# A hybrid decoder layer: output norm by pairs of heads, last residual rows on TensorE, an earlier SiLU of z, transposes copied by VectorE

## The chip, the cores and the metric

The kernel runs on one core of one Trainium2 chip. The metric is the device time of one execution in microseconds (us); lower is better. Before the change three runs gave 1408.13, 1408.22 and 1409.44 us, median 1408.22.

A core has five engines, each with its own instruction stream executed in order: TensorE (PE in the profile, with PEld for its weight loads), VectorE (DVE), ScalarE (ACT), GpSimd (POOL) and SyncE (SP, which here only starts transfers). They meet through semaphores. Matmul results land in the accumulator memory (PSUM, tiles named ps_...), all else lives in on-chip SBUF tiles.

## The reference, cut to what matters

One layer of a decoder for 256 prompt tokens and 8 samples of 4 tokens, 288 tokens together, width 2048:

```python
mix = concat[A(z_A), B(z_B), C(z_C)]          # z = rms_norm(x) @ w_in
x   = x + rms_norm(mix @ w_out, g_post_mix)
x   = x + rms_norm(relu(rms_norm(x) @ w_up) ** 2 @ w_down, g_post_mlp)
```

A is dilated attention, C sliding-window attention, B a gated delta rule with 4 heads of 128. The change touches three pieces of B and the last line:

```python
o = rms_norm(o, dn_g) * silu(b_z)             # B's output norm, per head, and its gate z
S = S * gl + kd^T @ v_new                     # state; for the samples written to state_delta_s
y = x + rms_norm(u @ w_down, g_post_mlp)      # the last residual, 16 rows of 128 x 288
```

## The kernel before, in words

All tensors are held transposed: 128 features on the partitions, 288 tokens along the free dimension, so a "row" of the residual is a tile of 128 x 288 and the layer has 16 of them. Every weight matmul is done in three passes: the weights come by DMA in pieces (`base_wr`), ACT casts a piece to a rounded high part (`base_wh`, line 384), DVE subtracts to get the low part (`base_wl`, line 326), and PE adds high x high, high x low and low x high into one accumulator (line 316). The pieces run one after the other: `w_in` (88 pieces), `w_o1` (32, over the first 12 of the 16 mixed rows, those of A and C and of nothing that B makes), `w_o2` (8, over B's 4 rows), then `w_up` and `w_dn`. At piece i the program casts piece i+3 and makes the low part of piece i+2.

B's own work is written as generators (`g_group`, `g_chunk`, `g_bdec`, `g_bfin` ...). A generator does a step and yields an estimated latency; between pairs of matmuls `advance` takes each generator that is due and emits its next step. So the order on each engine is fixed when the program is built, by those latencies, and the hardware keeps it.

The places that the change touches:

- `g_group(kind)`: convolved queries (kind 0), keys (1) and values (2) get their SiLU on ACT, between two loads of ACT's function table. In kind 2 the same function also takes the SiLU of the gate z (`zs`, 128 x 1152) and, after the second table load, multiplies it by the norm's gain `dng`.
- `inverse4`: the triangular inverse of a chunk. PE transposes `U` into a PSUM tile (`ps_mx`), ACT copies it to `A` (`b_cAA`), DVE makes the masked start matrices `b_cM` from it.
- `g_bdec`: the samples' chunk. At its end it multiplies the 8 tiles of old state `s0` (`st_s`, 128 x 512) by their decay on POOL; much later, during the `w_up` pieces, `fill_out` adds PE's update on DVE and stores the tile.
- `g_bfin`: B's output norm. It must be done before the last piece of `w_o1`, since `split_mix` turns its result (`base_mix` rows 6 to 9) into the high and low parts that `w_o2` reads.
- The tail after the last matmul: a sum of squares by two matmuls with a matrix of ones, ACT's Ln and Exp, three DVE instructions (`newton`) that refine 1/sqrt into `ml_m_r`, and then for each row of y a multiplication by `ml_m_r` and an addition of the residual row, DVE on rows 0 to 10 in groups, POOL on rows 15 down to 11 one at a time, and the stores from SP and ACT.

PSUM has 8 buffers: 2 `ps_acc`, 2 `ps_lx`, 4 `ps_mx`. A buffer is reused when its last reader is done.

## Time and profile before

| | |
|---|---|
| median of 3 runs | 1408.22 us |
| the profiled execution's own time | 1408.04 us |
| its span, first to last instruction | 1406.3 us |
| busy: PE / DVE / ACT / POOL | 1365.2 / 789.7 / 589.7 / 137.7 us |
| mean granted TensorE clock | 0.992 |

The profile shows one execution. Busy time is time in which an engine executes. Timeline rows read: start, duration, engine, source line, operation, out<-in, shape, how many merged, and in brackets the idle time just before with the instruction that ended it. Rows of the windows view give, for a stretch A:B, its length and each engine's busy time with the number of instructions, then the granted TensorE clock (1.00 is full speed) and the use of the DMA engines. Group rows end with busy us, mean ns of one | idle before.

### The profile page before, as it was taken

Reading aid. Unit: us, or ns where it says so; the run is one execution under the profiler, and the core shown is the slowest. Engines: PE = TensorE matmul, PEld = TensorE weight load, DVE = VectorE, ACT = ScalarE, POOL = GpSimd, SP = SyncE. Lnnn points to the kernel's source line nnn. Section 1 sums busy time; section 2 is a strip of 40 time slices with the busy share of each in tenths; the row PEclk is TensorE's granted clock in tenths of the full one; section 3 lists DMA queues with packets and bytes.
Section 4 is the critical chain, followed back from the end, with each engine's and each line's share of the span. In section 5 each row is a group of like instructions: output and inputs, shape, how many; then the busy total and the mean of one; then the engine's idle time right before and its main releaser. Section 6 shows DMA issues by size and latency. Waiting matters only on the chain.

```text
span 1406.3 us, 26913 instructions
## 1 busy us (share of the span) xinstructions
PE 1365.2 (97%) x11293; PEld 1301.2 (93%) x11293; DVE 789.7 (56%) x1302; ACT 589.7 (42%) x901; POOL 137.7 (10%) x203
## 2 busy tenths in 40 slices
PE   8999999999989999999999999999999999999994
PEld 7888887789978989899999999999999999999994
DVE  7543455546876667976433555443555444555555
ACT  7443434434772346633333334333433333434441
POOL 1111110102440050000000000000000000000114
PEclk9999999999999999999999999999999999999997
DMA  7779888744423536555555454545454545455541
GB/s 273 286 289 355 315 315 320 278 155 155 143 84 93 157 98 234 171 180 186 180 166 165 150 172 158 180 154 177 153 176 157 174 161 169 157 173 164 167 151 67
DMA packets 71065, 262.12 MB, mean 186 GB/s; under 512 B 8128, under 2 KB 10560, under 8 KB 70944
## 3 DMA queue, kind: packets, MB, share of 16 engines
q1 hardware_dynamic: 68544, 254.72, 53.8%
q0 software_dynamic: 1536, 4.89, 0.9%
q8 instruction: 88, 1.44, 0.4%
q10 hardware_dynamic: 864, 0.80, 0.2%
q14 instruction: 33, 0.27, 0.1%
HBM read 253.14 MB, written 7.24 MB: 185 GB/s over the span
## 4 chain that ended last, share of the span: by engine, by line
PE 91%; DVE 5%; ACT 2%; issue 1%; POOL 1%; DMA 0%; SPq 0%; POOLq 0%; DVEq 0%; ACTq 0%
PE ps_acc L316 35%; PE ps_mx L316 33%; PE ps_lx L316 21%; DVE base_wl L326 1%; PE ps_mx L320 1%; POOL ml_y L326 1%; DVE base_mix L326 1%; DMA base_wr<-w_in 0%; DVE b_cM L326 0%; DVE base_xl L335 0%; DVE cv_sq L335 0%; ACT base_xh L1534 0%; DVE base_xl L326 0%; DVE x_sa L326 0%; ACT base_mix L323 0%
## 5 line engine op out<-in xcount | busy, mean ns | idle before, releaser
L384 ACT CAST base_wh<-base_wr 128x1024 fp32r<-128x1024 f32 (+1 forms) x374 | 385.2, 1032 | 551.7 <-PE ps_mx L316 207.2
L326 DVE TENSOR_TENSOR base_wl<-base_wr,base_wh 128x1024 fp32r<-128x1024 f32 (+1 forms) x376 | 458.4, 1233 | 75.6 <-ACT base_wh L384 74.3
L316 PE MATMUL ps_acc<-base_xh,base_wh 128*128 128x288 f32 (+1 forms) x1056 | 322.1, 306 | 1.0 <-DVE at_z L335 0.8
L316 PE MATMUL ps_acc<-base_xl,base_wh 128*128 128x288 f32 (+1 forms) x1056 | 310.8, 296 | 0.7 <-DVE base_xl L326 0.7
L316 PE MATMUL ps_acc<-base_xh,base_wl 128*128 128x288 f32 x1040 | 303.9, 295 | 2.8 <-DVE base_wl L326 2.8
L316 PEld LDWEIGHTS ps_acc<-base_xh,base_wh 128*128 128x128 f32 (+1 forms) x1056 | 197.5, 187 | 19.0 <-issue 15.9
L316 PE MATMUL ps_mx<-ml_big,base_wh 128*128 128x288 f32 x1024 | 203.3, 294 | 0.0
L316 PEld LDWEIGHTS ps_acc<-base_xl,base_wh 128*128 128x128 f32 (+1 forms) x1056 | 197.5, 187 | 2.0 <-DVE base_xl L326 1.0
L316 PEld LDWEIGHTS ps_acc<-base_xh,base_wl 128*128 128x128 f32 x1040 | 194.9, 188 | 3.7 <-DVE base_wl L326 3.7
L316 PEld LDWEIGHTS ps_mx<-ml_big,base_wh 128*128 128x128 f32 x1024 | 164.1, 188 | 0.0
L316 PE MATMUL ps_mx<-ml_big,base_wl 128*128 128x288 f32 x512 | 150.9, 295 | 0.0
L316 PE MATMUL ps_mx<-base_xh,base_wh 128*128 128x288 f32 x480 | 142.3, 296 | 0.0
L316 PE MATMUL ps_mx<-base_xl,base_wh 128*128 128x288 f32 x480 | 141.6, 295 | 0.0
L316 PE MATMUL ps_mx<-base_xh,base_wl 128*128 128x288 f32 x480 | 141.1, 294 | 0.0
L316 PE MATMUL ps_lx<-base_xh,base_wh 128*128 128x288 f32 x400 | 122.7, 307 | 5.9 <-ACT base_xh L323 5.9
L316 PE MATMUL ps_lx<-base_xh,base_wl 128*128 128x288 f32 x400 | 116.1, 296 | 3.4 <-DVE base_wl L326 3.4
L316 PE MATMUL ps_lx<-base_xl,base_wh 128*128 128x288 f32 x400 | 118.9, 300 | 0.0
L316 PE MATMUL ps_acc<-ml_big,base_wh 128*128 128x288 f32 x512 | 101.8, 294 | 0.0
L316 PE MATMUL ps_lx<-ml_big,base_wh 128*128 128x288 f32 x512 | 101.8, 294 | 0.0
L316 PEld LDWEIGHTS ps_mx<-ml_big,base_wl 128*128 128x128 f32 x512 | 96.2, 188 | 0.0
L316 PEld LDWEIGHTS ps_mx<-base_xh,base_wl 128*128 128x128 f32 x480 | 90.4, 188 | 0.0
L316 PEld LDWEIGHTS ps_mx<-base_xl,base_wh 128*128 128x128 f32 x480 | 90.1, 188 | 0.1
(413 smaller groups left out, 1815.8 us busy)
## 6 DMA issues: line engine op xcount, KB each, us to landing
base_wr<-w_up SPq DMA_DIRECT2D x128, 512.0 KB, 3.7
base_wr<-w_dn SPq DMA_DIRECT2D x128, 512.0 KB, 3.8
base_wr<-w_in SPq DMA_DIRECT2D x86, 512.0 KB, 4.3
kv_kv<-kv_k SPq DMA_DIRECT2D x24, 896.0 KB, 7.8
kv_kv<-kv_v SPq DMA_DIRECT2D x28, 768.0 KB, 7.0
base_wr<-w_o SPq DMA_DIRECT2D x32, 384.0 KB, 3.1
base_wr<-w_o SPq DMA_DIRECT2D x8, 512.0 KB, 4.5
ml_big<-xT SPq DMA_DIRECT2D x4, 576.0 KB, 4.9
```

The source lines that it names most:

```text
L316: PE.matmul(out, lhsT=lhsT, rhs=rhs, start=start, stop=stop, **kw)
L320: PE.transpose(out, in_, idn)
L326: eng.tensor_tensor(out=out, in0=a, in1=b, op=op)
L384: S.copy(out=p["wh"], in_=p["wr"])
```

## The change

It has five parts.

1. The SiLU of z moves from the values' group to the keys' group, between that group's own table loads, and the multiplication by `dng` leaves ACT (it is folded into the norm's last instruction).
2. `inverse4` copies the transposed `U` on DVE instead of ACT (one copy of 128 x 512 for each of the two chunks).
3. The decay of the sample states leaves POOL: instead of 8 multiplications there and 8 additions on DVE, DVE does 4 fused multiply-adds of 128 x 128 per tile in `fill_out`.
4. `g_bfin` works by pairs of heads. POOL no longer takes part; DVE multiplies z by o, reads the sums of squares straight from PSUM, and does three fused instructions of 128 x 576 per pair. ACT's four PSUM copies and its second Square are gone, Exp is done per pair. `split_mix` of B's rows is issued in two halves.
5. The tail: PE adds the residual for rows 9 to 15. Seven PSUM buffers are first filled with identity x residual row, then identity x scaled row is added, ACT copies the sum back and stores it (3, 2 and 2 rows per store). DVE scales rows 9 to 15, then scales and adds rows 0 to 8 itself, stored by SP in groups of 4, 2, 2 and 1. POOL has no part in it.

The diff, without the constant `BY_PE = (9, 10, 11, 12, 13, 14, 15)`:

```diff
@@ g_group
-        if kind == 2:
+        if kind == 1:
             zs = mixp[:, 6:10, :]
             act(zs, zs, AF.Silu)
+            done.add("siluz")
         ...
         S.preload_act_table_set("natural_log_exp_and_others")
-        if kind == 2:
-            act(zs, zs, AF.Identity, scale=dng)
-            done.add("siluz")
@@ inverse4
-        S.copy(out=A, in_=p)
+        V.tensor_copy(out=A, in_=p)
@@ g_bdec
-        fill.update(vn=vn, kd=kds, s0=s0)
-        for i in range(8):
-            ...
-            tt(G, t, t, bc(sc, [P, 4, P]), ALU.mult)
-            yield FP
+        fill.update(vn=vn, kd=kds, s0=s0, eg=eg3)
@@ fill_out
-        tt(V, t, t, p.rearrange("p (n x) -> p n x", n=4), ALU.add)
+        for n in range(4):
+            k = 8 * h + 4 * q + n
+            stt(V, t[:, n, :], t[:, n, :], fill["eg"][:, k:k + 1], p[:, n * P:(n + 1) * P], ALU.mult, ALU.add)
@@ g_bfin
-        act(sq, B["o"], AF.Square)
-        tt(G, zs, zs, B["o"], ALU.mult)
-        ...
-            act(r[:, h, :], p, AF.Ln, bias=epsc[:, 0:1], scale=1.0 / P)
-            S.copy(out=t[:, h, :], in_=p)
-        ...
-        act(r, r, AF.Exp, scale=-0.5)
-        act(sq, r, AF.Square)
-        tt(G, zs, zs, r, ALU.mult)
-        stt(V, t, t, EPS * P, sq, ALU.add, ALU.mult)
-        ts(V, t, t, -0.5 / P, ALU.mult, 1.5, ALU.add)
-        tt(V, zs, zs, t, ALU.mult)
+        pairs = (slice(0, 2), slice(2, 4))
+        for a in pairs:
+            act(sq[:, a, :], B["o"][:, a, :], AF.Square)
+        tt(V, zs, zs, B["o"], ALU.mult)
+        yield 1.5
+        for a in pairs:
+            for h in range(a.start, a.stop):
+                p = mx(T)
+                mm(p, ones, sq[:, h, :])
+                act(r[:, h, :], p, AF.Ln, bias=epsc[:, 0:1], scale=1.0 / P)
+                cur["bf", h] = p
+            act(r[:, a, :], r[:, a, :], AF.Exp, scale=-0.5)
+            if a.start == 0:
+                yield 0.4
+        for a in pairs:
+            for h in range(a.start, a.stop):
+                stt(V, t[:, h, :], cur.pop(("bf", h)), EPS * P, r[:, h, :], ALU.add, ALU.mult)
+            ta, ra, za = t[:, a, :], r[:, a, :], zs[:, a, :]
+            stt(V, ta, ta, -0.5 / P, ra, ALU.mult, ALU.mult)
+            stt(V, ta, ta, 1.5, ra, ALU.add, ALU.mult)
+            stt(V, za, za, dng, ta, ALU.mult, ALU.mult)
+            yield 2.5
         while "o1" not in done:
             yield 1.0
-        split_mix(range(N_P1, KT))
+        split_mix(range(N_P1, N_P1 + 2))
+        yield 0.8
+        split_mix(range(N_P1 + 2, KT))
@@ the tail
-        p = mx(T)
+        p = new_acc()[:, 0:T]
         ...
+        banks = {m: new_acc()[:, 0:T] for m in BY_PE}
+        for m in BY_PE:
+            mm(banks[m], ident, orow(m), stop=False)
         newton(V, r, t, p, r, 1.0 / D, EPS)
-        for steps in (((V, 0, 4, SP), (G, 15, 1, S)), ((V, 4, 2, SP), (G, 14, 1, S)), ((V, 6, 3, SP), (G, 13, 1, S)),
-                      ((V, 9, 1, SP), (G, 12, 1, S)), ((V, 10, 1, SP), (G, 11, 1, S))):
-            ...
+        def by_pe(lo, n):
+            for m in range(lo, lo + n):
+                mm(banks[m], ident, y[:, m, :], start=False)
+                S.copy(out=y[:, m, :], in_=banks[m])
+            out(S, lo, n)
+        scale(9, 2)
+        scale(11, 1)
+        by_pe(9, 3)
+        scale(12, 4)
+        by_pe(12, 2)
+        by_pe(14, 2)
+        for lo, n in ((0, 4), (4, 2), (6, 2), (8, 1)):
+            scale(lo, n)
+            add(lo, n)
+            out(SP, lo, n)
```

Three places where the instructions of an engine stand in another order. The names carry buffer numbers, which differ by one or two between the programs; so do source lines.

ACT at the values' group, before the change (`base_mix` is z here, `cv_ca` a convolved value, `base_pm` holds `dng`):

```order
L648 ACT_TABLE_LOAD
L323 ACTIVATE base_mix_65<-base_mix_65 128x1152
L323 ACTIVATE cv_ca_4442<-cv_ca_4442 128x312
L323 ACTIVATE cv_ca_4517<-cv_ca_4517 128x312
L323 ACTIVATE cv_ca_4610<-cv_ca_4610 128x312
L323 ACTIVATE cv_ca_4753<-cv_ca_4753 128x312
L655 ACT_TABLE_LOAD
L323 ACTIVATE base_mix_65<-base_mix_65,base_pm_62 128x1152
L384 CAST base_wh_4816<-base_wr_4665 128x768
L384 CAST base_wh_4858<-base_wr_4744 128x768
L812 COPY b_cAA_32_4899<-ps_mx_4903 128x512
L812 COPY b_cAA_35_4930<-ps_mx_4934 128x512
```

and after it:

```order
L649 ACT_TABLE_LOAD
L324 ACTIVATE cv_ca_4443<-cv_ca_4443 128x312
L324 ACTIVATE cv_ca_4518<-cv_ca_4518 128x312
L324 ACTIVATE cv_ca_4611<-cv_ca_4611 128x312
L324 ACTIVATE cv_ca_4754<-cv_ca_4754 128x312
L657 ACT_TABLE_LOAD
L385 CAST base_wh_4815<-base_wr_4666 128x768
L385 CAST base_wh_4857<-base_wr_4745 128x768
L385 CAST base_wh_4948<-base_wr_4781 128x768
```

Both instructions on z are gone from between the table load and the cast of the next weight piece, and both copies are gone from behind it.

DVE in the output norm, before the change (`sp_ft`, `sp_fa`, `sp_fb` are the norm's temporaries, `base_oext` takes a finished row of `w_o1`):

```order
L326 TENSOR_TENSOR base_wl_6120<-base_wr_5962,base_wh_6119 128x768
L326 TENSOR_TENSOR base_wl_6155<-base_wr_6006,base_wh_6154 128x768
L1538 COPY base_mix_65<-ps_lx_6160 128x288
L326 TENSOR_TENSOR base_wl_6189<-base_wr_6082,base_wh_6188 128x768
L335 SCALAR_TENSOR_TENSOR sp_ft_6137<-sp_ft_6137,sp_fa_6109 128x1152
L332 TENSOR_SCALAR sp_ft_6137<-sp_ft_6137 128x1152
L326 TENSOR_TENSOR base_wl_6216<-base_wr_6123,base_wh_6215 128x768
L1538 COPY base_oext_66<-ps_acc_6221 128x288
L326 TENSOR_TENSOR base_mix_65<-base_mix_65,sp_ft_6137 128x1152
L326 TENSOR_TENSOR base_wl_6245<-base_wr_6158,base_wh_6244 128x768
```

and after it:

```order
L336 SCALAR_TENSOR_TENSOR sp_ft_6109<-ps_mx_6137,sp_fb_6108 128x288
L336 SCALAR_TENSOR_TENSOR sp_ft_6109<-ps_mx_6140,sp_fb_6108 128x288
L336 SCALAR_TENSOR_TENSOR sp_ft_6109<-sp_ft_6109,sp_fb_6108 128x576 x2
L336 SCALAR_TENSOR_TENSOR base_mix_65<-base_mix_65,base_pm_62,sp_ft_6109 128x576
L327 TENSOR_TENSOR base_wl_6120<-base_wr_5961,base_wh_6119 128x768
L327 TENSOR_TENSOR base_wl_6164<-base_wr_6005,base_wh_6163 128x768
L336 SCALAR_TENSOR_TENSOR sp_ft_6109<-ps_mx_6151,sp_fb_6108 128x288
L336 SCALAR_TENSOR_TENSOR sp_ft_6109<-ps_mx_6154,sp_fb_6108 128x288
L336 SCALAR_TENSOR_TENSOR sp_ft_6109<-sp_ft_6109,sp_fb_6108 128x576 x2
L336 SCALAR_TENSOR_TENSOR base_mix_65<-base_mix_65,base_pm_62,sp_ft_6109 128x576
L1537 COPY base_mix_65<-ps_lx_6169 128x288
L327 TENSOR_TENSOR base_wl_6189<-base_wr_6081,base_wh_6188 128x768
```

The norm's DVE work now stands two to three weight pieces earlier, around the low parts `wl_6120` and `wl_6164` and ahead of `wl_6189`, in ten instructions where there were three.

DVE in the tail, before the change:

```order
L326 TENSOR_TENSOR ml_y_8004<-ml_y_8004,ml_m_r_15129 128x1152
L326 TENSOR_TENSOR ml_y_8004<-ml_y_8004,base_mix_65 128x1152
L326 TENSOR_TENSOR ml_y_8004<-ml_y_8004,ml_m_r_15129 128x576
L326 TENSOR_TENSOR ml_y_8004<-ml_y_8004,base_mix_65 128x576
L326 TENSOR_TENSOR ml_y_8004<-ml_y_8004,ml_m_r_15129 128x864
```

and after it:

```order
L327 TENSOR_TENSOR ml_y_8022<-ml_y_8022,ml_m_r_15147 128x576
L327 TENSOR_TENSOR ml_y_8022<-ml_y_8022,ml_m_r_15147 128x288
L327 TENSOR_TENSOR ml_y_8022<-ml_y_8022,ml_m_r_15147 128x1152 x2
L327 TENSOR_TENSOR ml_y_8022<-ml_y_8022,base_mix_65 128x1152
L327 TENSOR_TENSOR ml_y_8022<-ml_y_8022,ml_m_r_15147 128x576
L327 TENSOR_TENSOR ml_y_8022<-ml_y_8022,base_mix_65 128x576
L327 TENSOR_TENSOR ml_y_8022<-ml_y_8022,ml_m_r_15147 128x576
L327 TENSOR_TENSOR ml_y_8022<-ml_y_8022,base_mix_65 128x576
```

Seven rows are scaled first (576, 288 and the first 1152), for PE; then come rows 0 to 8, scaled and added.

## The prediction

> **What bounds the kernel now.** I read the chain of waits first, then PE's rows that stood idle, then the windows around them, then the rows of the engines that PE waited for.

> ```profile
> PE 91%; DVE 5%; ACT 2%; issue 1%; POOL 1%; DMA 0%; SPq 0%; POOLq 0%; DVEq 0%; ACTq 0%
> ```

> PE carries 91% of the chain that ended last. An edit on another engine is worth only the time that PE stands idle for it, or what stands behind the last matmul. The change touches three such places, and all else that it moves lies beside PE.

> ```profile
> 421.85 0.66 PE L320 MATMUL ps_mx<-base_cst,cv_ca 128*128 128x128 f32 x2 [4.18 <-DVE b_cB L326]
> 518.89 0.40 PE L316 MATMUL ps_acc<-base_xh,base_wl 128*128 128x288 f32 x1 [1.24 <-DVE base_wl L326]
> 522.72 0.40 PE L316 MATMUL ps_lx<-base_xh,base_wl 128*128 128x288 f32 x1 [1.18 <-DVE base_wl L326]
> 525.92 0.40 PE L316 MATMUL ps_lx<-base_xh,base_wl 128*128 128x288 f32 x1 [0.54 <-DVE base_wl L326]
> 1386.61 0.75 PE L316 MATMUL ps_mx<-ml_sq,base_cst 128*128 128x288 f32 x2 [0.59 <-ACT ml_sq L323]
> ```

> PE waits 4.18 us for DVE at the values' group (place A), 1.24 + 1.18 + 0.54 = 2.96 us for low parts at the output norm (place B), and after 1387.36 it has nothing more to do while the residual is added (place C). The profiled execution took 1408.04 us, 1.74 more than its span of 1406.3 and 0.18 less than the median.

> **Place A: the SiLU of z and the two copies.**

> ```profile
> 414.24 1.17 ACT L323 ACTIVATE base_mix<-base_mix 128x1152 f32<-128x1152 f32 x1
> 415.31 1.51 ACT L323 ACTIVATE cv_ca<-cv_ca 128x312 f32<-128x312 f32 x4
> 418.13 1.25 ACT L323 ACTIVATE base_mix<-base_mix,base_pm 128x1152 f32<-128x1152 f32 x1
> 419.30 1.55 ACT L384 CAST base_wh<-base_wr 128x768 fp32r<-128x768 f32 x2
> ...
> 420.14 0.96 DVE L326 TENSOR_TENSOR base_wl<-base_wr,base_wh 128x768 fp32r<-128x768 f32 x1 [4.48 <-ACT base_wh L384]
> 421.62 1.12 DVE L335 SCALAR_TENSOR_TENSOR b_cU<-ps_mx,b_bP,b_cA 128x128 f32<-128x128 f32 x4
> 431.81 0.28 DVE L326 TENSOR_TENSOR b_cM<-ps_mx,base_cst 128x128 f32<-128x128 f32 x1
> ```

> Start to start, z's SiLU holds ACT for 415.31 − 414.24 = 1.07 us and its product with `dng` for 419.30 − 418.13 = 1.17. Without both, the cast starts at 417.06 instead of 419.30, and DVE's low part, which stands in order ahead of `b_cB`, 2.24 us earlier. So PE's stall falls from 4.18 to about 1.95 us. Whether that reaches the end depends on who is the bound next.

> ```profile
> 417.66:421.85 4.19, 0.01 (x2) 0.03 (x1) 1.71 (x3) 3.65 (x5) 2.52 (x7) 0.90 0.11 40
> 421.85:427.20 5.35, 5.07 (x21) 4.64 (x22) 5.16 (x19) 1.32 (x2) 0.00 (x0) 0.50 0.23 74
> 427.20:434.40 7.20, 7.04 (x168) 6.55 (x167) 7.04 (x18) 1.67 (x2) 0.00 (x0) 0.96 0.35 101
> ...
> 432.15 0.72 PE L316 MATMUL ps_mx<-b_cM 32*32 32x32 f32 x62 [0.16 <-DVE b_cM L326]
> ```

> Behind the stall PE runs 5.35 us at a granted clock of 0.50, with few long matmuls (21). DVE is busy for 5.16 of those 5.35 us and 7.04 of the next 7.20, and at 432.15 PE waits for DVE again. So DVE, not the slow clock, sets the pace from 420.14 to 432: it starts 2.24 us earlier, but it now also makes the two copies of 128 x 512 out of PSUM, each 0.68 us alone and about 0.60 from start to start (the `st_s` row under place B; `b_cB` to `b_cU`: 421.02 to 421.62). Gain at A: 2.24 − 1.2 = 1.0; I take **0.9**, since POOL is busy for 2.52 us in the first window and may hold DVE a little. Bounds: 0 if DVE's extra work comes in front of something that PE needs at once; above, the case in which PE is the bound there (a rival, below).

> The moved SiLU adds its 1.07 us to ACT in the keys' group. The next low part there comes later by as much:

> ```profile
> 382.54 1.23 DVE L326 TENSOR_TENSOR base_wl<-base_wr,base_wh 128x1024 fp32r<-128x1024 f32 x1 [1.10 <-ACT base_wh L384]
> 380.00:400.00 20.00, 19.91 (x143) 19.09 (x142) 16.31 (x29) 13.37 (x25) 9.86 (x21) 1.00 0.40 125
> ```

> It would be done at 383.77 + 1.07 = 384.8. Low parts are made two pieces ahead, and PE was idle for only 0.09 of these 20 us, so I cost this at nothing; with the cover gone, at most 1.1.

> **Place B: the output norm.**

> ```profile
> 498.09 0.96 DVE L326 TENSOR_TENSOR base_wl<-base_wr,base_wh 128x768 fp32r<-128x768 f32 x1 [1.14 <-ACT base_wh L384]
> ...
> 510.60 2.89 DVE L326 TENSOR_TENSOR base_wl<-base_wr,base_wh 128x768 fp32r<-128x768 f32 x1
> 513.42 2.19 DVE L335 SCALAR_TENSOR_TENSOR sp_ft<-sp_ft,sp_fa 128x1152 f32<-128x1152 f32 x1
> 515.64 1.48 DVE L332 TENSOR_SCALAR sp_ft<-sp_ft 128x1152 f32<-128x1152 f32 x1
> 517.04 1.79 DVE L326 TENSOR_TENSOR base_wl<-base_wr,base_wh 128x768 fp32r<-128x768 f32 x1
> 519.13 1.83 DVE L326 TENSOR_TENSOR base_mix<-base_mix,sp_ft 128x1152 f32<-128x1152 f32 x1
> ...
> 509.99 2.68 POOL L326 TENSOR_TENSOR base_mix<-base_mix,sp_fb 128x1152 f32<-128x1152 f32 x1 [4.42 <-ACT sp_fb L323]
> 512.63 7.11 POOL L326 TENSOR_TENSOR st_s<-st_s,st_eg 128x512 f32<-128x512 f32 x4
> ```

> One low part of 128 x 768 takes 0.96 us alone (498.09) and 2.89 and 1.79 while POOL computes (from 509.99 on). That, with the norm's three instructions (2.19 + 1.48 + 1.83 = 5.5 us) in front, is why PE waits. After the change POOL has no norm product and no decay, only two masks that the order puts ahead, so DVE runs at its own speed. What it gets:

> ```profile
> L326 DVE TENSOR_TENSOR base_mix<-base_mix,ml_big 128x576 f32<-128x576 f32 x5 | 3.8, 758 | 0.2
> L335 DVE SCALAR_TENSOR_TENSOR ml_r<-ps_lx,ml_m_r 128x288 f32<-128x288 f32 x1 | 0.5, 458 | 0.2 <-ACT ml_m_r L323 0.2
> L326 DVE TENSOR_TENSOR st_s<-st_s,ps_mx 128x512 f32<-128x512 f32 x4 | 2.6, 681 | 0.0
> ...
> 515.10 0.29 PE L316 MATMUL ps_acc<-base_xh,base_wl 128*128 128x288 f32 x1
> ```

> Four instructions of 128 x 288 from PSUM (0.46), six of 128 x 576 (0.76) and one of 128 x 1152 (1.36, the row 1389.89 under C): 1.8 + 4.6 + 1.4 = 7.8 us, 2.3 more than before, but on a free DVE. By the new order the product goes ahead at about 499.9, when POOL made it before; the first pair follows near 505 to 508, the low parts 6120 by 508.9 and 6164 by 509.8, the second pair to 512.9, low part 6189 by 514.1. In the old trace PE begins six matmuls on each of these parts, at 0.40 us each, the third at 515.10 (the first two at 510.3 and 512.7). So the tightest (6120 and 6189) have 1.4 and 1.0 us left, and from 514.1 DVE runs ahead of PE. The sums of squares now stay in PSUM until DVE has read them, in `ps_mx` buffers that `w_o1` (`ps_acc`, `ps_lx`) does not use. All three stalls go: **2.9**, with 3.0 as the most. Downward, with that slack gone, each us that DVE is later costs PE a us; if all 7.8 us came in front of the low parts, the place would lose 7.8 − 3.0 = 4.8 and its clock with it.

> [...]

> **The additions of the sample states** become four instructions per tile: 1.12 us (421.62) in place of 0.68, 0.44 x 8 = 3.5 us on DVE. Cover:

> ```profile
> 607.95 0.46 DVE L335 SCALAR_TENSOR_TENSOR ml_m_t<-ps_mx,ml_m_r 128x288 f32<-128x288 f32 x1 [6.07 <-ACT ml_m_r L323]
> ```

> The additions are spread over the first `w_up` pieces, where DVE stands idle for 6.07 us in front of this row alone. Nothing; with no cover, one tile in front of a waited-for part costs 0.44.

> **Place C: the tail.**

> ```profile
> 1389.89 1.36 DVE L326 TENSOR_TENSOR ml_y<-ml_y,ml_m_r 128x1152 f32<-128x1152 f32 x1
> 1391.28 1.83 DVE L326 TENSOR_TENSOR ml_y<-ml_y,base_mix 128x1152 f32<-128x1152 f32 x1
> ...
> 1390.02 1.88 POOL L326 TENSOR_TENSOR ml_y<-ml_y,ml_m_r 128x288 f32<-128x288 f32 x1 [8.86 <-DVE ml_m_r L335]
> 1402.38 0.88 POOL L326 TENSOR_TENSOR ml_y<-ml_y,base_mix 128x288 f32<-128x288 f32 x1
> ...
> 559.52 1.13 PE L316 MATMUL ps_lx<-ml_sq,base_cst 128*128 128x288 f32 x4
> ```

> Both engines work from 1389.89 to 1403.26, and the last store lands 3.04 us later, at the span's end. They slow each other: DVE's 1152 row takes 1.83 in place of 1.36 once POOL has begun. After the change DVE has, at their own lengths, 0.76 (rows 9, 10), 0.46 (11), 1.36 (12 to 15), 2 x 1.36 (0 to 3), 4 x 0.76 (4 to 7) and 2 x 0.46 (8): 9.3 us. Independent neighbours overlap by some 0.1 us (the seven here about 0.6), dependent ones stand 0.03 apart, so the last addition ends near 1389.89 + 9.3 − 0.5 = 1398.7 instead of 1403.26: 4.56 us. PE's part must end before that. One fp32 matmul of 128 x 288 is two instructions, so the row 559.52 holds two of them: 0.57 us each. The seven fills, 4.0 us, stand from 1387.4 beside Ln, Exp and the refinement; the seven additions follow the scaled rows, which are there from 1391 and complete near 1392.3, and end near 1395.3, ACT's last copy (some 0.4) at 1396. At half clock they would end near 1399.5 and take 0.8 of the gain, but between fills and additions PE hardly stands idle. The stores (three from ACT behind its copies, four from SP, for five each) have nothing queued behind them. The store of row 8 is as small as the last one before, but 2.36 MB now leave in a shorter time: 0 to 1 us more for the landing, I take 0.15. **4.4**, bounds 2 and 4.6.

> **Sum.** 0.9 + 2.9 + 4.4 = 8.2; 1408.04 − 8.2 = 1399.8, plus 0.18 to the median: **1400.0 us**.

> **Rivals.**

> *All of A comes through (1396).* If PE and its clock, not DVE, bound 421.85 to 432, the whole 2.24 counts, and a stall of 1.95 us may leave the clock up, as stalls of 1.24 did elsewhere:

> ```profile
> 500.00:520.00 20.00, 18.76 (x135) 18.11 (x134) 12.50 (x10) 10.90 (x17) 15.57 (x10) 1.00 0.27 81
> ```

> The 5.35 us at 0.50 would then give 2.7 back: 4.9 in place of 0.9. For it speaks the 0.50; against it DVE's 5.16 of 5.35 us. [...]

> *The stores bound the tail (1402).* If the last store waits for those ahead of it, C gives half, 2.2. For it: 16 rows end within 5 us; against it: in the old tail the DMA engines were used to 0.41.

> *The norm's stalls only move (1403 to 1406).* DVE's ten instructions delay low parts 6120 to 6189 past their slack, and new stalls eat the 2.9 or a little more: 1408.2 − 0.9 − 4.4 = 1402.9, and up to 3 us above that. For it: 7.8 us of DVE work between 505 and 513; against it: DVE idled for 5.44 us before 504.49 and 2.98 before 510.23 there.

> ```profile
> 504.49 0.46 DVE L1538 COPY base_mix<-ps_lx 128x288 f32<-128x288 f32 x1 [5.44 <-PE ps_lx L316]
> 510.23 0.46 DVE L1538 COPY base_mix<-ps_lx 128x288 f32<-128x288 f32 x1 [2.98 <-PE ps_lx L316]
> ```

> *Slower (1411).* The same mechanism whole: the first pair starts late, all 7.8 us stand in front of a low part, PE idles over 4 us, and the clock falls as behind 417.66: 5.35 us at 0.50 and 0.58 more in the next window (0.04 x 7.20 / 0.5) cost 3.0. If PE at place A waits for DVE's copies too, 0.4 is left there. 4.8 + 3.0 − 0.4 − 4.4 = +3.0. It decides once B loses more than the 5.3 us of A and C. For it speaks that DVE already has 5.5 us of norm work where PE now waits; against it, DVE's gaps above.

> **Chances.** Forecast 0.62, all of A 0.12, stores 0.14, moved stalls 0.08, slower 0.04. The forecast's own range is 1398 to 1402; to hold 8 in 10 it must reach into the first and third rival: **1396.5 to 1403.5**. A measurement here tells about 0.2% (2.8 us, so 1405.4 and 1411.0) from no change. Half of the moved stalls and a little of the slower case lie within it: faster 0.91, same 0.05, slower 0.04.

> **What would show it.** A: PE's stall before the values' transposes about 2 us instead of 4.2, clock not at 0.50, DVE without idle up to the masked start matrices. B: no PE row from 510 to 530 that waits for `base_wl`, low parts at 0.96 instead of 2.89, POOL without 128 x 1152. C: the last DVE addition 8.8 us after the refinement, the span's end 3 us behind it, no POOL row. Wrong: a PE stall on a low part near 512 to 516; low parts still near 2 us; a DVE gap in the tail; a last store that lands over 4 us after the last addition.

## The result and the profile after

The changed kernel takes **1398.99 us** (median of 4 runs, 1398.06 to 1400.43) against 1408.33 us before (4 runs beside it, 1408.13 to 1409.44): a ratio of 0.9935, 95% interval 0.9923 to 0.9946. Two later measurements gave 1400.21 (0.9945, 0.9932 to 0.9957) and 1399.81 us (0.9944, 0.9931 to 0.9956). So it is 8 to 9 us faster. The first trace of it has a span of 1397.8 us, 8.5 less than the trace before the change.

To see where that went, both programs need the same landmarks. VectorE copies each finished mixed row out of PSUM (line 1538 before, 1537 after). The first, fourth, sixth, eleventh and fifteenth of these copies in the stretch serve here. VectorE's timeline before and, behind the dots, after (start, duration, instruction):

```profile
412.71 0.45 DVE L1538 COPY base_mix<-ps_acc 128x288 f32<-128x288 f32 x1
440.57 0.46 DVE L1538 COPY base_mix<-ps_lx 128x288 f32<-128x288 f32 x1 [0.63 <-PE ps_lx L316]
459.26 0.45 DVE L1538 COPY base_mix<-ps_acc 128x288 f32<-128x288 f32 x1
528.35 0.46 DVE L1538 COPY base_oext<-ps_lx 128x288 f32<-128x288 f32 x1 [0.38 <-PE ps_lx L316]
```

```profile
412.17 0.45 DVE L1537 COPY base_mix<-ps_acc 128x288 f32<-128x288 f32 x1
439.02 0.46 DVE L1537 COPY base_mix<-ps_lx 128x288 f32<-128x288 f32 x1 [0.63 <-PE ps_lx L317]
458.99 0.45 DVE L1537 COPY base_mix<-ps_acc 128x288 f32<-128x288 f32 x1
504.21 0.46 DVE L1537 COPY base_mix<-ps_lx 128x288 f32<-128x288 f32 x1 [2.29 <-PE ps_lx L317]
524.37 0.46 DVE L1537 COPY base_oext<-ps_lx 128x288 f32<-128x288 f32 x1 [2.61 <-PE ps_lx L317]
```

| stage, by landmarks of before | before | after | gain |
|---|---|---|---|
| 0 to 412.71 (nothing changed but the moved SiLU) | 412.71 | 412.17 | 0.54 |
| 412.71 to 440.57, values' group and start of the inverse (A) | 27.86 | 26.85 | 1.01 |
| 440.57 to 459.26, rest of the inverse | 18.69 | 19.97 | -1.28 |
| 459.26 to 504.49 | 45.23 | 45.22 | 0.01 |
| 504.49 to 528.35, output norm (B) | 23.86 | 20.16 | 3.70 |
| 528.35 to the span's end, with the tail (C) | 877.95 | 873.43 | 4.52 |

The first line is no gain: the twelve later traces, of kernels with and without the moved SiLU, have 412.10 to 413.48 there. B and C delivered a little more than forecast. A delivered its 1.0 us and, in this trace, lost it within the next 20 us.

TensorE's timeline after, the longest waits in A and behind it; from 446 to 560 us no row waited 0.15 us or more, so the three waits for low parts at B are gone:

```profile
419.11 0.41 PE L321 MATMUL ps_mx<-base_cst,cv_ca 128*128 128x128 f32 x2 [1.98 <-DVE b_cB L327]
430.61 0.72 PE L317 MATMUL ps_mx<-b_cM 32*32 32x32 f32 x62 [1.62 <-DVE b_cM L327]
445.65 0.23 PE L317 MATMUL ps_mx<-b_cM 32*32 32x32 f32 x3 [1.68 <-issue]
```

and the same matmul, with another that stopped, before:

```profile
446.45 0.23 PE L316 MATMUL ps_mx<-b_cM 32*32 32x32 f32 x3 [0.89 <-issue]
453.90 0.22 PE L316 MATMUL ps_mx<-b_cM,b_cAA 32*32 32x32 f32 x2 [0.68 <-issue]
```

The stall of 4.18 us fell to 1.98, as worked out. Between the first two rows stand three more waits for VectorE, of 0.54, 0.84 and 0.79 us, where the profile before has one of 0.28; VectorE itself has no idle row from 417.40 to 432 us. "issue" says that TensorE waited for no engine and no data transfer that the profile shows. Behind the longer one, at 445.65, the clock fell. Windows of the changed kernel, the third number from the right being the granted clock:

```profile
439.28:442.69 3.41, 3.41 (x115) 3.20 (x114) 2.45 (x5) 0.68 (x2) 0.00 (x0) 1.00 0.60 194
442.69:446.10 3.41, 1.73 (x101) 1.41 (x100) 0.35 (x2) 0.59 (x1) 0.00 (x0) 1.00 0.43 137
446.10:449.51 3.41, 3.41 (x19) 3.33 (x14) 0.77 (x3) 0.00 (x0) 0.00 (x0) 0.50 0.02 5
```

In the last of them the granted clock was 0.50, and TensorE's matmuls of 128x288 started every 0.24 us (446.93 to 449.33) where they start every 0.13 at 1.00. So it did in 3.41 us what takes about 1.9 at 1.00, an estimate from these rows. That loss of 1.5 us, and 0.1 more of stops than before (1.68 against 0.89 + 0.68), is more than what A had won.

The norm on VectorE, after: pairs and low parts at their own lengths, with GpSimd silent (0.95 for a low part where it took 2.89):

```profile
504.67 0.82 DVE L336 SCALAR_TENSOR_TENSOR sp_ft<-ps_mx,sp_fb 128x288 f32<-128x288 f32 x2
505.53 1.55 DVE L336 SCALAR_TENSOR_TENSOR sp_ft<-sp_ft,sp_fb 128x576 f32<-128x576 f32 x2
507.12 0.82 DVE L336 SCALAR_TENSOR_TENSOR base_mix<-base_mix,base_pm,sp_ft 128x576 f32<-128x576 f32 x1
507.85 1.82 DVE L327 TENSOR_TENSOR base_wl<-base_wr,base_wh 128x768 fp32r<-128x768 f32 x2
...
513.13 0.95 DVE L327 TENSOR_TENSOR base_wl<-base_wr,base_wh 128x768 fp32r<-128x768 f32 x1
```

The tail after, VectorE's first and last group and ScalarE's last copies, then the window from VectorE's last addition to the span's end:

```profile
1385.94 3.67 DVE L327 TENSOR_TENSOR ml_y<-ml_y,ml_m_r 128x576 f32<-128x576 f32 x4
1390.73 0.70 ACT L1947 COPY ml_y<-ps_mx 128x288 f32<-128x288 f32 x2 [0.41 <-PE ps_mx L317]
1394.32 0.46 DVE L327 TENSOR_TENSOR ml_y<-ml_y,base_mix 128x288 f32<-128x288 f32 x1
```

```profile
1394.78:1397.80 3.02, 0.00 (x0) 0.00 (x0) 0.00 (x1) 0.00 (x0) 0.00 (x0) 0.54 0.45 170
```

VectorE needs 1394.78 - 1385.94 = 8.84 us in place of the 13.4 that it and GpSimd needed together, ScalarE is done at 1391.4, and the span ends 3.02 us behind the last addition (3.04 before).

### The profile page after: what moved, and what is told of

Its sections match the earlier page's. It is cut to its first block, busy times and chain, and to the rows that moved or that the text cites. A ratio compares the mean times of both kernels' runs of the same rounds, so it can differ in the third digit from the quotient of the medians.

```text
span 1397.8 us, 26979 instructions
## 1 busy us (share of the span) xinstructions
PE 1370.3 (98%) x11321; PEld 1304.6 (93%) x11321; DVE 787.8 (56%) x1337; ACT 588.3 (42%) x902; POOL 107.2 (8%) x183
## 3 DMA queue, kind: packets, MB, share of 16 engines
q8 instruction: 88, 1.44, 0.4%
## 4 chain that ended last, share of the span: by engine, by line
PE 91%; DVE 5%; issue 1%; ACT 1%; DMA 0%; POOL 0%; SPq 0%; DVEq 0%; ACTq 0%; POOLq 0%
PE ps_acc L317 35%; PE ps_mx L317 34%; PE ps_lx L317 21%; PE ps_mx L321 1%; DVE base_wl L327 1%; DVE base_xl L336 1%; DVE ml_y L327 1%; DMA x_xt<-xT 0%; DVE base_mix L327 0%; DVE x_sa L327 0%; DVE b_cM L327 0%; DVE cv_sq L336 0%; ACT base_xh L1533 0%; DVE cv_ca L336 0%; ACT ml_m_r L324 0%
```

## The experiments

### Each part alone, and the whole again

`e1_only_a` has parts 1 and 2, `e2_only_b` parts 3 and 4, `e3_only_c` part 5, each put into the kernel before. Since the gain `dng` belongs to part 1 and is used in part 4, it is moved so:

```diff
 # parts 1 and 2 alone: the norm as before, the gain in its last instruction
-        tt(V, zs, zs, t, ALU.mult)
+        stt(V, zs, zs, dng, t, ALU.mult, ALU.mult)
 # parts 3 and 4 alone: the gain stays in the values' group
-            stt(V, za, za, dng, ta, ALU.mult, ALU.mult)
+            tt(V, za, za, ta, ALU.mult)
```

> Parts 1 and 2 alone (z's SiLU with the keys, the gain folded into the norm's last instruction, the two copies by VectorE), all else as before. Theory 1 (what the trace of the changed kernel shows): VectorE reaches the first 128x128 start matrix about 1.0 us earlier than before, but TensorE then runs out of instructions near 444 us (a stall of 1.5 to 1.8 us that ends on no other engine's work) and its clock halves for 3.4 us, so that by 459 us nothing is left: 1408.0 to 1408.6 us. Rival (the prediction's term): 0.9 us stays, 1407.4 us. Rival 2 (all of the earlier start): 1403 to 1404 us.

> Parts 3 and 4 alone (no decay and no norm product on GpSimd, the norm by pairs), z's SiLU and gain as before. Theory 1: the three waits for low parts go, and with each the restart of TensorE behind it, together 3.7 us, so 1404.6 us, and no row of TensorE between 505 and 530 us that waits for base_wl. Rival (the prediction's term): 2.9 us, 1405.4 us. Rival 2: stalls of the same length elsewhere, 1407 us or more.

> Part 5 alone, the tail. Theory 1: VectorE's last addition ends 8.9 us after the refinement's last instruction in place of 13.4, and the span's end stays 3.0 us behind it: 4.55 us, 1403.8 us. Rival: the stores, which now leave closer together, push the end out by 1 us or more: 1404.8 us or later, with the end of the span over 4 us behind the last addition.

> The changed kernel again, for its interval beside the parts and for a second trace. Theory 1: 1399.0 us, and the stall of TensorE near 444 us with the halved clock behind it is there again, since the order of the instructions is fixed. Rival: the stall depends on where the transfers of weights happen to stand, and differs in length or place between two executions, with 0 to 2.5 us between them.

| | time, us | ratio to before (95%) |
|---|---|---|
| A alone | 1407.11 | 0.9996 (0.9987 to 1.0004) |
| B alone | 1404.50 | 0.9974 (0.9965 to 0.9984) |
| C alone | 1403.24 | 0.9968 (0.9955 to 0.9980) |
| all, second measurement | 1400.21 | 0.9945 (0.9932 to 0.9957) |

before beside them: 1408.12. B and C each clear the noise, A alone does not. Since runs of one kernel spread over 1.5 to 2.8 us, the stage lengths of the traces say more (with the later runs, explained below):

| trace | 412 to 440 | 440 to 459 | 459 to 504 | 504 to 528 | 528 to end |
|---|---|---|---|---|---|
| before | 27.86 | 18.69 | 45.23 | 23.86 | 877.95 |
| B alone (e2) | 27.83 | 18.92 | 45.23 | 20.16 | 878.19 |
| C alone (e3) | 27.86 | 18.52 | 45.22 | 23.84 | 873.16 |
| A alone (e1) | 26.83 | 19.20 | 45.23 | 23.84 | 877.95 |
| all, first trace | 26.85 | 19.97 | 45.22 | 20.16 | 873.43 |
| all, second trace (e4) | 26.85 | 20.57 | 45.22 | 20.17 | 873.43 |
| all, third trace (e11) | 26.84 | 19.05 | 45.22 | 20.17 | 873.39 |
| all, copies on ScalarE (e7) | 25.62 | 18.46 | 45.22 | 20.16 | 873.50 |
| the same again (e10) | 25.63 | 19.82 | 45.23 | 20.16 | 873.56 |
| the same, nine rows in the tail (e12) | 25.66 | 19.41 | 45.23 | 20.16 | 873.61 |
| all, tail on VectorE (e9) | 26.86 | 19.48 | 45.23 | 20.17 | 875.60 |
| all, decay on GpSimd (e8) | 28.24 | 18.49 | 45.21 | 21.80 | 873.45 |
| all, program shifted (e5) | 28.20 | 16.48 | 45.61 | 20.17 | 873.42 |
| all, eight weight pieces not fetched (e6) | 28.22 | 19.32 | 44.14 | 20.17 | 873.37 |

B gives 3.70 in every trace that has it whole, to a few hundredths, and C, with its tail unchanged, 4.4 to 4.8. A gives 1.0 up to 440 in e1, e4, e9, e11 and the first trace, and the next stage is then longer than in the kernels without A (19.05 to 20.57 against 18.52 to 18.92). Over both stages the three kernels without A have 46.38 to 46.75, mean 46.56, and the five traces with it (and no other edit there) 45.89 to 47.42, mean 46.50: on average nothing is left, though the spread would hide some tenths. (The 28.2 us of e5, e6 and e8 hold an event of the same kinds before 440: a stop at 436.69, and a fall of the clock at 432.1 and 431.2.)

For B and C theory 1 held, in the time and in the trace. For A alone it held in part. VectorE's 1.0 us came, but the stop was 0.89 us long and the clock did not fall behind it, 0.52 us of the gain was still there at 459 us (46.03 against 46.55), and 1407.11 us lies nearer to the rival's 1407.4 than to 1408.0; the interval, 1406.3 to 1408.7 us, holds both. In the second trace of the whole change the stop came again (1.73 us), and so did the fall of the clock behind it; the time was 1.2 us above the 1399.0 expected.

The rest of the stretch confirms what sets the pace in A up to 440. In e4 and e11 the clock fell at 419.5 and 420.5, in the first trace it did not, and the length is 26.85, 26.84 and 26.85. So VectorE, not TensorE's clock, was the bound there.

### What TensorE waits for behind A: its own program

In A alone TensorE stops three times with "issue". Its timeline, and the windows from one stop to the next (TensorE's matmuls and weight loads with their counts are the first two columns behind the length):

```profile
446.09 0.23 PE L316 MATMUL ps_mx<-b_cM 32*32 32x32 f32 x3 [0.89 <-issue]
450.09 0.38 PE L316 MATMUL ps_mx<-b_cM 32*32 32x32 f32 x20 [0.67 <-issue]
453.82 0.22 PE L316 MATMUL ps_mx<-b_cM,b_cAA 32*32 32x32 f32 x2 [0.42 <-issue]
```

```profile
0.00:446.00 446.00, 430.39 (x3905) 375.60 (x3906) 266.73 (x611) 208.70 (x418) 85.99 (x154) 1.00 0.66 240
446.00:450.00 4.00, 3.33 (x128) 3.02 (x128) 1.63 (x5) 0.83 (x1) 0.00 (x0) 1.00 0.10 37
450.00:453.60 3.60, 3.30 (x128) 2.99 (x128) 1.97 (x4) 0.00 (x0) 0.00 (x0) 1.00 0.19 34
```

128 + 128 = 256 instructions lie between two stops, both times. Before the change, after it and here, the first stop comes behind 3905 matmuls and 3906 loads, the same place in the program (7811; the trace has 62 other instructions of TensorE by then, hence 7873 in the expectations). The queue "q8 instruction" of the profile moved 16 KB at a time (88 packets and 1.44 MB before the change and after it), and in this stretch one such transfer starts every 3.4 to 5.6 us here. Two experiments test this.

The first shifts the program against its blocks: 24 tiny matmuls, about 96 instructions, ahead of everything.

```diff
+        pz = mx(T)
+        for _ in range(24):
+            mm(pz[0:32, 0:32], sa0[0:32, 0:32], sa0[0:32, 0:32])
         load_part(0, 0, 256)
```

> The changed kernel with 24 small fp32 matmuls of 32x32x32 ahead of TensorE's first one, where it waits 5.2 us anyway; all that follows stands about 96 of TensorE's instructions later in its stream. In the two traces of the changed kernel TensorE stops at its instructions 7873 and 8385 (counted from its first, weight loads included), with no engine to wait for, and in the part-1-and-2 run also at 8129: 256 apart each. Theory 1 (TensorE waits for its next 16 KB of program, 256 instructions): the stops are again at 7873, 8129 or 8385 of the new count, so at other matmuls of the program, and together shorter: 0.6 to 1.0 us in place of 1.7 to 2.3, and if the clock then stays up, TensorE is done with the stretch from the start of the tables to 459 us 1.5 to 3 us earlier. Rival (the matmul that stops waits for its data): the stop stays with the same matmul, now counted 7969, and is as long as before.

TensorE's rows with "issue" from 415 to 460 us in it, and the windows up to the first and from there to the second stop:

```profile
436.69 0.31 PE L318 MATMUL ps_mx<-b_cM 32*32 32x32 f32 x10 [1.14 <-issue]
455.15 0.33 PE L318 MATMUL ps_mx<-b_cM 32*32 32x32 f32 x16 [0.31 <-issue]
```

```profile
0.00:436.60 436.60, 423.85 (x3650) 369.84 (x3650) 260.79 (x598) 206.12 (x414) 85.99 (x154) 1.00 0.67 243
436.60:455.10 18.50, 18.16 (x639) 16.82 (x640) 11.08 (x26) 4.87 (x8) 1.29 (x2) 1.00 0.28 89
```

The stops are at other matmuls, none of them the old one. They lie 1279, about 5 x 256, apart, and the first stands 7300 instructions in, 511 or two blocks ahead of the old 7811. (The two counts are one short of whole blocks; I take it that a record of a matmul is missing there.) The rival, by which the stop stays with its matmul, falls. I had named the blocks at 7873 to 8385; the stops were at the blocks 7361 and 8641 of the same grid. Together they took 1.45 us, not 0.6 to 1.0. The two stages took 44.68 us, 1.2 to 2.7 less than in the three traces of the changed kernel, and the time was 1398.25 us (0.9934, 0.9922 to 0.9947), which its interval cannot tell from the 0.9935 to 0.9945 of the changed kernel.

The second asks why a fetch is late. It takes the weight transfers out of the way:

```diff
-            SP.dma_start(out=p["wr"], in_=p["src"])
+            if p["n"] == 768 and 11 <= n_o1 <= 18:     # counted over the w_o1 pieces
+                G.memset(p["wr"], 0.0)
+            else:
+                SP.dma_start(out=p["wr"], in_=p["src"])
```

> The changed kernel with eight weight pieces of w_o1, those that are fetched from about 428 to 456 us, set to zero by GpSimd in place of their transfers (so these weights are left out of the result). Theory 1a (the program's 16 KB are fetched late because the weights occupy the DMA engines): the fetch that started 2.4 us after TensorE passed its instruction 7617 starts about 1.0 us after it, the stop at 7873 shrinks from 1.7 to 0.6 us or less, and the clock does not fall behind it. Rival (1b: the fetch has its own delay, weights or not): the fetch again starts 1.5 to 2.5 us after 7617 and the stop is 1.3 us or more.

The stop that took 1.68 and 1.73 us:

```profile
446.85 0.23 PE L317 MATMUL ps_mx<-b_cM 32*32 32x32 f32 x3 [0.20 <-issue]
```

TensorE's clock stayed up behind it. Counted in the traces, the fetch that belongs to this border starts 0.95 us after TensorE passes instruction 7617, one block earlier. In the thirteen traces where weights travel it starts 1.3 to 2.5 us after it (1.50 before; 2.44, 2.51 and 2.24 in the three traces of the changed kernel; 1.79 in A alone). From the start of that transfer to TensorE's next instruction it is 2.2 to 2.5 us wherever TensorE stops at this border, 2.38 here. The first trace of the changed kernel shows the same without an edit. These are its windows from the entry into a block to the start of the next fetch, at 7617 and one block later; the last two numbers are the use of the DMA engines and GB/s:

```profile
440.83:443.28 2.45, 2.45 (x96) 2.24 (x82) 1.58 (x3) 0.83 (x1) 0.00 (x0) 1.00 0.58 167
445.65:446.69 1.04, 1.04 (x41) 1.00 (x40) 0.62 (x2) 0.00 (x0) 0.00 (x0) 0.72 0.00 0
```

So theory 1a holds: with the eight weight pieces out of the way the fetch starts 0.95 us after 7617 in place of 2.24 to 2.51 in the changed kernel. When it is asked for no trace shows. The weights are not all of it. The next two borders of the kernel without these weights still stopped TensorE for 0.40 and 0.69 us, with the DMA engines idle ahead of the fetch. The time of this kernel (1400.79 us, one run) tells nothing of a gain, since its clock fell twice elsewhere (at 421.9 and 432.1).

This is what A ran into: TensorE comes 1.0 us earlier to a stretch of 32x32 matmuls, in which 256 instructions (2.95 us from 7617 on in the first trace, 440.83 to 443.78) last less than it takes to the start of the next fetch and from there to TensorE's next instruction (2.45 + 2.37 us there, 0.95 + 2.38 without the weights). The stops are there without A too. At the same border, with B alone and with C alone:

```profile
446.57 0.23 PE L316 MATMUL ps_mx<-b_cM 32*32 32x32 f32 x3 [1.41 <-issue]
446.21 0.23 PE L317 MATMUL ps_mx<-b_cM 32*32 32x32 f32 x3 [1.30 <-issue]
```

Added up from 440 to 459 us, the rows with "issue" hold 1.30 to 1.81 us in the three traces without A (mean 1.56) and 1.68 to 2.50 in the five with it (mean 2.09). In two of these five the clock also fell behind the stop, and the 256 instructions there took 4.6 to 4.7 us in place of 3.5 to 4.0. Half a us of longer stops, and about 1 us in two traces of five, make roughly the 1.0 that is lost on average. This is a tally of eight traces. Why the stops are longer after an earlier arrival stays open: the fetch started 1.8 to 2.5 us after 7617 with A and 1.5 to 2.2 without, and the ranges overlap.

### The copies back on ScalarE

```diff
-        V.tensor_copy(out=A, in_=p)
+        S.copy(out=A, in_=p)
```

> The changed kernel with the two copies of the transposed U back on ScalarE. Theory (VectorE sets the pace from 417 to 431 us): without its two copies VectorE reaches the first 128x128 start matrix 1.2 us earlier than in the changed kernel, TensorE's waits for b_cM there shrink from 2.3 us by as much; but the time of the whole gains less, 0 to 1 us, since TensorE's stops for its program are next: 1398.5 to 1400 us. Rival (ScalarE's own work or TensorE sets the pace there): VectorE reaches that matrix at the same time or later.

> The changed kernel with the two copies on ScalarE, again, beside the changed kernel in the same stretch of time. Theory 1 (part 2 costs 1.2 us of VectorE where VectorE sets the pace): VectorE reaches its first 128x128 start matrix 2.2 us earlier than before the change and 1.2 earlier than with the whole change; in the time, after TensorE's stops for its program, 0.5 to 2.5 us below the changed kernel. Rival: the first trace of it was only lucky with the clock, and the times are equal within 0.5 us.

> The changed kernel, third look. Theory 1: VectorE's first 128x128 start matrix 1.0 us earlier than before the change, a stop at TensorE's instruction 7873 of 1.2 to 1.8 us, the clock at half for none, one or two stretches of 3.41 us between 415 and 450 us, and 1398.5 to 1400.5 us.

The first stage takes 25.62 and 25.63 us, 1.22 less than with the copies on VectorE: that part of both expectations holds, and the 2.24 us that the prediction worked out for part 1 stand in full (27.86 - 25.62). TensorE's waits for `b_cM` there fell from 3.2 to 2.0 us. Behind it the two traces differ, 18.46 with no fall of the clock and 19.82 with one (at 445.53, behind a stop of 1.44 us). The times were 1397.49 us (0.9931, 0.9919 to 0.9944) the first time, 1.0 below the range that was expected, and 1399.42 us (0.9934, 0.9920 to 0.9947) the second, against 1399.81 us of the changed kernel beside it. One of the five runs of the second time took 4688.70 us and is left out of the ratio, its cause is not known; the median of the other four is 1398.72. So the second pair decides neither for 0.5 to 2.5 us nor for equal times, for the intervals overlap. Without that one run, the 14 on record with the copies on ScalarE (those of the last kernel below among them) have a median of 1398.1 us, and the 14 of the changed kernel 1399.8; they were not all taken side by side. The third trace of the changed kernel came out as expected: a stop of 1.54 us, one stretch of half clock, 1399.81 us. So part 2 by itself costs 1.2 us on VectorE where VectorE is the bound, and its place in the change is paid by part 1's 2.2.

### What GpSimd's absence is worth at the norm

```diff
 # g_bdec and fill_out as before the change, all else as after it
+            tt(G, t, t, bc(sc, [P, 4, P]), ALU.mult)          # 8 times
-            stt(V, t[:, n, :], t[:, n, :], fill["eg"][:, k:k + 1], p[:, n * P:(n + 1) * P], ALU.mult, ALU.add)
+        tt(V, t, t, p.rearrange("p (n x) -> p n x", n=4), ALU.add)
```

> The changed kernel with the decay of the sample states on GpSimd again (8 multiplications there, 8 plain additions on VectorE later), all else as changed. Theory 1 (GpSimd's work slows VectorE's): GpSimd's multiplications lie beside the norm by pairs, VectorE's 128x576 instructions and low parts there take 1.3 to 2 times their length, TensorE waits for base_wl again between 505 and 520 us, 1 to 4 us in all: 1400 to 1403 us. Rival (the gain is that of the order by pairs and the earlier start): no wait of over 0.3 us, 1399 to 1400 us.

GpSimd's, VectorE's and TensorE's timelines of it (GpSimd's two masks follow its decay, to 510.01):

```profile
497.09 9.87 POOL L327 TENSOR_TENSOR st_s<-st_s,st_eg 128x512 f32<-128x512 f32 x8
...
500.00 1.36 DVE L327 TENSOR_TENSOR base_mix<-base_mix,b_oB 128x1152 f32<-128x1152 f32 x1 [2.89 <-ACT b_oB L1035]
501.28 1.79 DVE L327 TENSOR_TENSOR base_wl<-base_wr,base_wh 128x768 fp32r<-128x768 f32 x1
505.12 0.82 DVE L336 SCALAR_TENSOR_TENSOR sp_ft<-ps_mx,sp_fb 128x288 f32<-128x288 f32 x2
505.97 3.13 DVE L336 SCALAR_TENSOR_TENSOR sp_ft<-sp_ft,sp_fb 128x576 f32<-128x576 f32 x2
509.13 1.48 DVE L336 SCALAR_TENSOR_TENSOR base_mix<-base_mix,base_pm,sp_ft 128x576 f32<-128x576 f32 x1
...
511.54 0.40 PE L317 MATMUL ps_acc<-base_xh,base_wl 128*128 128x288 f32 x1 [0.90 <-DVE base_wl L327]
516.81 0.40 PE L317 MATMUL ps_acc<-base_xh,base_wl 128*128 128x288 f32 x1 [0.22 <-DVE base_wl L327]
```

While GpSimd works, two instructions of 128x576 take 3.13 us in place of 1.55, the third 1.48 in place of 0.82, and a low part 1.79 in place of 0.95. TensorE waits 0.90 and 0.22 us again, and the stage takes 21.80 in place of 20.16: of B's 3.70 us, 1.64 hang on the decay alone. Theory 1 holds, the time (1403.82 us, 0.9972, 0.9963 to 0.9981) being 0.8 above what I had written; the part of it that the norm's stage does not explain stays open. The pair that reads PSUM (505.12) is not slowed, and neither is the product of 128x1152 (500.00), which reads two tiles of SBUF; why that one escapes stays open.

### The tail

```diff
 # VectorE alone
-        scale(9, 2)  ...  by_pe(14, 2)
-        for lo, n in ((0, 4), (4, 2), (6, 2), (8, 1)):
+        for lo, n in ((0, 4), (12, 4), (4, 2), (6, 3), (9, 2), (11, 1)):
```

> The changed kernel with the tail on VectorE alone: 16 rows scaled and added there (groups of 4, 4, 2, 3, 2, 1), no identity matmuls, nothing on GpSimd. Theory 1 (VectorE alone, at its own 0.34 us per row and step, sets the tail): 32 row steps in place of 25, 7 x 0.34 = 2.4 us more, so 1401 to 1402 us, and still about 2 us less than with GpSimd's help in the old tail. Rival (what the tail won was GpSimd's absence alone, TensorE's part hides what VectorE would do anyway): within 0.5 us of the changed kernel.

Its last addition:

```profile
1397.04 0.46 DVE L327 TENSOR_TENSOR ml_y<-ml_y,base_mix 128x288 f32<-128x288 f32 x1
```

VectorE needs 11.26 us for the rows (1386.24 to 1397.50) against 8.84 with TensorE's help, 2.42 more, as expected, and the kernel takes 1402.21 us (0.9959, 0.9945 to 0.9972), 0.2 above the expected range. In the last stage it has 875.60, between 877.95 and 873.43: of C's 4.52 us, 2.35 come from GpSimd's leaving VectorE alone and 2.17 from TensorE's taking seven additions.

The last kernel goes further that way and has the copies on ScalarE too:

```diff
         by_pe(14, 2)
-        for lo, n in ((0, 4), (4, 2), (6, 2), (8, 1)):
+        scale(7, 2)
+        for m in (7, 8):
+            banks[m] = new_acc()[:, 0:T]
+            mm(banks[m], ident, orow(m), stop=False)
+        by_pe(7, 2)
+        for lo, n in ((0, 4), (4, 2), (6, 1)):
```

> The changed kernel with the two copies on ScalarE, and nine rows in place of seven added by TensorE in the tail (rows 7 and 8 in buffers that are free again after their copy). Theory 1: as the kernel with the copies on ScalarE, less two row additions of VectorE, 0.7 us: 1397 us. Rival (ScalarE's copies and its stores, now two rows longer, end the tail): no gain in the tail, or a last store later than VectorE's.

VectorE's last addition, the window from its end to the span's end, and its last store (its size and the time from issue to landing; 2.0 us for the store of one row in the changed kernel):

```profile
1392.39 0.46 DVE L327 TENSOR_TENSOR ml_y<-ml_y,base_mix 128x288 f32<-128x288 f32 x1
```

```profile
1392.85:1396.70 3.85, 0.00 (x0) 0.00 (x0) 0.00 (x0) 0.00 (x0) 0.00 (x0) 0.75 0.58 218
```

```profile
yT<-ml_y SPq DMA_DIRECT2D x1, 144.0 KB, 2.7
```

The rows are done 0.79 us sooner (8.05 in place of 8.84) and the end comes 0.83 later behind them (3.85 in place of 3.02). Of these 0.83, 0.7 is the longer way of the last store. The rival holds: nothing is won in the tail, the stores are next. It took 1398.14 us, 1.1 above the expected 1397 (ratio 0.9929, 0.9915 to 0.9943, the lowest of all), and with 1397.81 to 1398.51 below all five runs of the changed kernel beside it (1399.18 to 1401.60). I take its advantage from the copies on ScalarE, since the tail shows none; the intervals of the ratios overlap.

## Why the prediction was right, and where not

The forecast was 1400.0 us (1396.5 to 1403.5), the result 1398.99. Two of its steps were off by 0.8 to 0.9 us in opposite directions, so it is luck that the sum of 8.2 us is better than its terms.

- **Place A, 0.9 us: wrong as a term of the sum.** The step "DVE sets the pace from 420.14 to 432", with 2.24 saved and 1.2 paid for two copies, is exact: 27.86 became 26.85, and 25.62 without the copies. So the rival "all of A comes through" falls too, and its half clock cost nothing there. What failed is that I ended the account at 432, where TensorE waits for VectorE, and carried the 1.0 us to the end. Between 440 and 459 us TensorE waits for its program and sometimes loses its clock, and on average A's gain is gone (46.50 us for both stages against 46.56). The prediction's fences showed neither of the two "issue" rows of the profile before (446.45 and 453.90), which were the sign of it.
- **The moved SiLU, nothing:** borne out. No row of TensorE waited between 329 and 405 us in the trace after.
- **Place B, 2.9 us: the mechanism right, the term too small: 3.70.** VectorE's schedule came as replayed: low part 6120 at 508.8 (508.9 worked out), the second pair to 512.84 (512.9), low part 6189 at 514.08 (514.1). The missing 0.74 is what a stop costs beside its idle number, three times 0.25:

```profile
517.36 0.29 PE L316 MATMUL ps_acc<-base_xl,base_wh 128*128 128x288 f32 x1
...
519.13 0.29 PE L316 MATMUL ps_acc<-base_xh,base_wh 128*128 128x288 f32 x1
```

  Matmuls start every 0.13 us. After 517.36 the next was due at 517.49 and started at 518.89, and the one behind it 0.24 later in place of 0.13: 1.40 + 0.11 = 1.51 us lost, where the row says 1.24. With the decay on GpSimd two waits of 1.12 us together cost 1.64, the same 0.26 for each. The norm gave up a TENSOR_SCALAR of 128x1152, which took 1.48 us beside GpSimd. What one costs with GpSimd silent no row of that length shows; smaller rows of the profile before do:

```profile
322.50 0.30 DVE L330 TENSOR_SCALAR cv_ga<-cv_ga 8x288 f32<-8x288 f32 x1 [0.51 <-ACT cv_ga L323]
326.53 0.45 DVE L335 SCALAR_TENSOR_TENSOR cv_gd<-cv_gb,cv_ga 8x288 f32<-8x288 f32 x1 [0.99 <-ACT cv_ga L323]
```

  By 0.46 us for a length of 288 and 1.36 for 1152, about 0.16 us of VectorE's rows does not grow with the length; without it 0.14 us of this TENSOR_SCALAR is left and 0.29 of the other row. That is an estimate from these four rows. It changes no term of the sum, which has the fused rows at their full length.
- **The additions of the sample states, nothing:** the last stage of B alone is 878.19 against 877.95, so at most 0.24 us of the 3.5 is seen.
- **Place C, 4.4 us: right, 4.52.** The 8.8 us on VectorE (8.84), the 3 us to the span's end (3.02), no waiting of TensorE or its clock. One reading was loose: the last store before landed at 1405.08, 1.82 us behind the last addition, and not at the span's end; after the change it is 2.05, the 0.15 that was allowed and a little more. The rival of the stores did not come, but it is only 0.8 us away, as the kernel with nine rows showed.
- **The rivals of moved stalls and of a slower kernel** did not come: no wait for a low part between 505 and 530 us.

## What to carry to other kernels

Follow a gain past the point where the engine that it helps is waited for again, up to the next landmark that both programs share; a short stretch of small matmuls behind it can take all of it back (46.50 us with A against 46.56 without, over both stages). A wait with no releaser ("issue") in a stretch of small instructions is worth a count of instructions between two such waits (here 128 + 128) before any engine is made faster. And when two engines work side by side on rows in SBUF, measure each alone first: here VectorE alone did all 16 rows in 11.26 us, where VectorE and GpSimd together needed 13.4.
